# Where the weight combinations stand in VectorE's queue: behind the low part of the first half of the tile ahead

## The chip, the core and the metric

The kernel runs on one core of one Trainium2 chip. The metric is the device time of one execution in microseconds (us), lower is better. TensorE (PE in the profile, PEld for its weight loads), VectorE (DVE), ScalarE (ACT), GpSimd (POOL) and SyncE (SP, which issues most DMAs) each run their own queue of instructions in order.

## The reference

One layer of a hybrid block on 512 positions of width 2048, in float32: a norm, one wide input projection, two branches, and projections back.

```python
h = rmsnorm(x, norm1_w)
proj = einsum('bsd,de->bse', h, w_in)            # 2048 x 22592
q, k, v, g_ret, z, xbc, dt_raw, gate_r, gate_s = split(proj, offsets)
y_r = retention(q, k, v, positions) * silu(g_ret)          # 8 heads of 256
y_s = rmsnorm(ssd(xbc, dt_raw, ...) * silu(z), ssd_norm_w) # 64 heads of 64
merged = sigmoid(gate_r) * (y_r @ w_br_ret) + sigmoid(gate_s) * (y_s @ w_br_ssd)
return rmsnorm(x + merged @ w_out, norm_f_w)
```

Almost all of the arithmetic is in products of the activations (512 columns, kept transposed) with weight matrices.

## The kernel before

**A unit.** The function `unit` (L250) makes 256 output rows: a sum over 2048 inputs, taken in 8 steps k of 256 inputs. In most units a step is not the plain product of a 2x2 block matrix but the seven products of Strassen's scheme in Winograd's form (the table SEVEN): four 128x128 weight blocks are combined to seven, the activations likewise, and seven products of 128x128 by 128x256 stand for eight. Units called `plain` use the four blocks as they are, with 512 columns (FOUR).

**High and low parts.** Each float32 factor is split in a rounded high part and the rest, and each product is three matmuls: high by high (L213), high by low (L214), low by high (L215). So a seven-product step is 21 matmuls, a unit 168.

**What prepares the weights.** In `products` (L200) a weight tile `wf` (L221, three buffers) holds the blocks of two steps, its two halves. SP loads it with two DMAs (L227). VectorE makes the combinations of both halves at once with three instructions: L230 (two differences, 128x512), L232 (from the result of L230, 128x256) and L233 (from the result of L232, 128x256). Then for each half `split` (L147) lets ScalarE round it to `whi` (L148, 128x896, seven buffers) and VectorE subtract to get `wlo` (L149, 128x896, six buffers). ScalarE's rounding of a half reads all seven blocks, so it waits for L233; VectorE's low part waits for ScalarE's rounding of that half. A buffer of `wf` is free for the next load when the low part of its second half has been made; `whi` and `wlo` buffers when TensorE has done with that step.

**The order on TensorE in a unit.** Steps 0 to 4 run one after another; the last three steps (LAST, L245) run group by group, so that the accumulators `pb` or `att` end in three portions. Behind each portion VectorE and ScalarE combine the accumulators to the output `o` (L266 to L270).

**What sets the order.** The program is written without an order between units of work; the framework's scheduler lays the queues out, by priority and by its own model of when things end. The weights' preparation runs with a raised priority (`tc.high_priority(offset=PRIO)`, L219), so it stands ahead of where it is written. Once laid out, each queue's order is fixed. An ordering edge without a semaphore (`add_manual_dep` with NoSync, used so far by the class `InOrder`, L93) makes one instruction stand behind another in the same queue and costs no instruction.

**The stages.** A start (norm, rotary tables, first splits); retention, eight heads of four units (q, k, v, gate), with rotations, scores and group norms between; the SSD branch, eight groups g of seven units (B and C; x and z for two pairs of channel blocks; two gate units), with the convolutions (L590), scans (L635 to L675) and gates between; `w_br_ret`; the upper and the lower half of `w_br_ssd`, the latter with the merge (L726 to L729); `w_out` with the last norm. Each of the last four begins with new activations to be split, and runs a plain unit, six seven-product units and another plain unit (`w_out` ends in a form of its own).

Of the kernel before, what the change touches and what calls it, by code (L numbers as in the profile page):

```python
# [8 lines left out]
F32 = mybir.dt.float32  # L9
# [3 lines left out]
ALU = mybir.AluOpType  # L13
# [3 lines left out]
P = 128  # L17
# [110 lines left out]
def hybrid_block(tc, A, out):  # L128
    nc = tc.nc
    PE, ACT, DVE, POOL, SP = nc.tensor, nc.scalar, nc.vector, nc.gpsimd, nc.sync  # L130
# [6 lines left out]
    op = ctx.enter_context(tc.tile_pool(name="op", bufs=2))  # L137
# [8 lines left out]

    def split(dst_hi, dst_lo, src):  # L147
        ACT.copy(dst_hi, src)  # L148
        DVE.tensor_tensor(dst_lo, src, dst_hi.bitcast(F32), op=ALU.subtract)  # L149

# [8 lines left out]
    def high(k, x):  # L161
        return X[k][0][:, x, :] if isinstance(x, slice) or x < 4 else X[k][1][:, x - 4, :]

    def low(k, x):
        if isinstance(x, slice):
            return X[k][0][:, x.start + 4:x.stop + 4:x.step, :]
        return X[k][0][:, x + 4, :] if x < 4 else X[k][1][:, x - 1, :]
# [9 lines left out]
    def second_halves(room):  # L177

        for i in range(NP):
            f, g = R[i], room[i % 2]  # L180
            DVE.tensor_tensor(g[:, 0:2, :], f[:, 0:5:4, :], f[:, 2:3, :].to_broadcast([P, 2, 256]), op=ALU.add)
            DVE.tensor_tensor(g[:, 2, :], f[:, 3, :], g[:, 1, :], op=ALU.subtract)
            t = X[i][1] = hp.tile([P, 6, 256], F32R, name=f"b{i}", tag=f"b{i}")
            split(t[:, 0:3, :], t[:, 3:6, :], g)

    def pair_rows(f):
        return f[:, 0:4, :].rearrange("p (r h) t -> p r (h t)", r=2)

    def rows(src, i):
        return src[i * 256:(i + 1) * 256, :].rearrange("(r p) t -> p r t", p=P)  # L190
# [9 lines left out]
    def products(parts, pt, groups, PE=PE, after=None):  # L200


        started, ws = set(), []
        plain = groups is not SEVEN
        n = 4 if plain else 7

        def go(k, p):
            b, half, w, x = p
            hi, lo = ws[k]
            xh, xl = high(k, x), low(k, x)  # L210
            wh, wl = hi[:, w, :], lo[:, w, :]
            o = pt[b][:, half, :]
            PE.matmul(o, wh, xh, start=b not in started, stop=False, skip_group_check=True)  # L213
            PE.matmul(o, wh, xl, start=False, stop=False, skip_group_check=True)  # L214
            PE.matmul(o, wl, xh, start=False, stop=(k == NP - 1), skip_group_check=True)  # L215
            started.add(b)

        for k in range(NP):
            with tc.high_priority(offset=PRIO):  # L219
                if k % 2 == 0:  # L220
                    f2 = wp.tile([P, 2, 7, P], F32, name="wf", bufs=FB)  # L221
                    for m in range(2):
                        c = 0
                        v = pair_rows(f2[:, m])
                        for ap in parts:
                            w = ap.shape[-1]
                            SP.dma_start(out=v[:, :, c:c + w], in_=rows(ap, k + m))  # L227
                            c += w
                    if not plain:
                        DVE.tensor_tensor(f2[:, :, 4:6, :], f2[:, :, 1:3, :],  # L230
                                          f2[:, :, 0:1, :].to_broadcast([P, 2, 2, P]), op=ALU.subtract)
                        DVE.tensor_tensor(f2[:, :, 0, :], f2[:, :, 2, :], f2[:, :, 4, :], op=ALU.add)  # L232
                        DVE.tensor_tensor(f2[:, :, 6, :], f2[:, :, 3, :], f2[:, :, 0, :], op=ALU.subtract)  # L233
                f = f2[:, k % 2]
                hi = wp.tile([P, 7, P], F32R, name="whi", bufs=HB)
                lo = wp.tile([P, 7, P], F32R, name="wlo", bufs=LB)
                split(hi[:, :n, :], lo[:, :n, :], f[:, :n, :])
            ws.append((hi, lo))
            if k < NP - LAST:
                for g in groups:  # L240
                    for p in g:
                        go(k, p)
            if after and k == 1:
                after()
        for g in groups:  # L245
            for k in range(NP - LAST, NP):
                for p in g:
                    go(k, p)

    def unit(parts, alt=False, plain=False):  # L250

        if alt:
            pt = [att_tile().rearrange("p (h t) -> p h t", h=2) for b in range(4)]
        else:
            pt = [acc.tile([P, 2, 256], F32, name=f"pb{b}") for b in range(4)]
        products(parts, pt, FOUR if plain else SEVEN)
        o = op.tile([P, 4, 256], F32, name="o")
        with tc.high_priority():
            if plain:
                for c in range(2):  # L260
                    ACT.copy(o[:, 2 * c:2 * c + 2, :], pt[2 * c][:, 0:1, :].to_broadcast([P, 2, 256]))
                    DVE.tensor_tensor(o[:, 2 * c, :], pt[2 * c][:, 1, :], o[:, 2 * c, :], op=ALU.add)
                    DVE.tensor_tensor(o[:, 2 * c:2 * c + 2, :], pt[2 * c + 1], o[:, 2 * c:2 * c + 2, :], op=ALU.add)
            else:
                p1, u = o[:, 0, :], o[:, 0:4:3, :]
                ACT.copy(p1, pt[0][:, 0, :])  # L266
                DVE.tensor_tensor(o[:, 1:3, :], pt[1], p1[:, None, :].to_broadcast([P, 2, 256]), op=ALU.add)
                DVE.tensor_tensor(u, o[:, 2:3, :].to_broadcast([P, 2, 256]), pt[2], op=ALU.subtract)
                DVE.tensor_tensor(o[:, 2, :], o[:, 0, :], pt[2][:, 1, :], op=ALU.subtract)
                DVE.tensor_tensor(u, pt[3], u, op=ALU.add)  # L270
        flat = o.rearrange("p s t -> p (s t)")
        return flat[:, 512:], flat[:, :512]
# [212 lines left out]
    with tc.tile_pool(name="ret", bufs=1) as rp:  # L485
# [3 lines left out]
        for h in range(NH):  # L489
# [40 lines left out]
            for sb in range(TB):  # L530
                n = T - sb * P
# [38 lines left out]
    with tc.tile_pool(name="ssd", bufs=1) as sp:  # L570
# [30 lines left out]
        for g in range(NG):  # L601
# [14 lines left out]
            for jj in range(2):  # L616
# [5 lines left out]
                for e in range(2):  # L622
# [9 lines left out]
                    for c in range(TB):  # L632
# [6 lines left out]
                                       op=ALU.mult)  # L639
# [96 lines left out]
    with tc.tile_pool(name="fin", bufs=1) as fp:  # L736
# [50 lines left out]

        last_w = [w_o[:, D - 256:]]
        products(last_w, pt, PASSES[0], pe)
        t1, t0 = (t[:, :, h] for h in halves)  # L790
        act.copy(o[0][:, 0:2, :], pt[0])
        dve.tensor_tensor(t1, pt[1], t1, op=ALU.add)
        dve.tensor_tensor(t1, o[0][:, 0:2, :], t1, op=ALU.add)
        act.activation(o[0][:, 2:4, :], t1, AF.Square)
        dve.tensor_tensor(t0, o[0][:, 0:2, :], t0, op=ALU.add)
        products(last_w, pt, PASSES[1], pe, lambda: sums(0))
        finish(0)
        dve.tensor_tensor(t0, pt[2], t0, op=ALU.add)
# [44 lines left out]
```

## Time and profile before

| | |
|---|---|
| median of 3 runs | 2768.85 us (2766.91 to 2770.41) |
| the profiled execution's own time | 2769.07 us |
| its span, first to last instruction | 2767.2 us |
| TensorE busy | 2699.1 us, 98% of the span |
| TensorE's weight loads busy | 2567.6 us, 93% |
| VectorE busy | 2371.0 us, 86% |
| ScalarE busy | 1343.0 us, 49% |
| mean granted TensorE clock | 0.992 |

The execution lies 1.9 us above its span, and 0.2 us above the median of the runs. In the rows of the profile L149 is line 149 of the kernel; "out<-in" are tile names; "[0.35 <-ACT whi L148]" is idle time of the engine just before the instruction, and what ended it. In a row by window each engine has its busy time and its count of instructions; in a row of waits stand the total in us, the number of waits and the longest.

### The profile page before, as it was taken

The page shows a single profiled execution, that of the slowest core. Times are in us where ns is not written, and L with a number is a line of the kernel's source. Part 1 is how long each engine was busy: PE and PEld are TensorE (multiplying, and loading weights), DVE is VectorE, ACT ScalarE, POOL GpSimd, SP SyncE. Part 2 cuts the span into 40 slices and gives each one's busy share as a digit, 9 for nine tenths or more (in the row PEclk, how much of TensorE's full clock was granted, in tenths as well). Part 3 has the DMA queues.
Part 4 walks back from the last instruction along what each step waited for, and adds up shares of the span by engine and source line. Part 5 has one row for each costly group of instructions (what it writes and reads, how often), then busy time and mean ns, then how long its engine had stood idle before and what let it go on. Part 6 is the DMA issues. An engine that isn't in the chain of part 4 may idle for free.

```text
span 2767.2 us, 51984 instructions
## 1 busy us (share of the span) xinstructions
PE 2699.1 (98%) x20448; PEld 2567.6 (93%) x20448; DVE 2371.0 (86%) x3799; ACT 1343.0 (49%) x1923; POOL 175.2 (6%) x130
## 2 busy tenths in 40 slices
PE   6999999999999999999999999999999999999998
PEld 3799999999999999999999999999999989899898
DVE  8788888888878898898989888898889798898997
ACT  4334333343336555566565556556564353433453
POOL 0000000000000100000000000000000000011221
PEclk8999999999999999999999999999999999999999
DMA  4233333333333434343443434344464544557634
GB/s 141 77 96 92 115 100 107 96 100 103 104 112 107 141 108 127 121 129 121 128 142 120 136 108 128 116 132 126 131 200 144 192 155 141 179 169 230 203 123 138
DMA packets 339766, 362.46 MB, mean 131 GB/s; under 512 B 25152, under 2 KB 297792, under 8 KB 339520
## 3 DMA queue, kind: packets, MB, share of 16 engines
q1 hardware_dynamic: 319136, 325.05, 38.2%
q10 hardware_dynamic: 20384, 34.09, 3.3%
q8 instruction: 160, 2.62, 0.4%
q14 instruction: 86, 0.70, 0.1%
HBM read 321.56 MB, written 37.49 MB: 130 GB/s over the span
## 4 chain that ended last, share of the span: by engine, by line
PE 75%; DVE 11%; DMA 8%; issue 3%; ACT 1%; SPq 1%; POOL 0%; DVEq 0%; ACTq 0%; POOLq 0%
PE pb L215 21%; PE pb L214 21%; PE pb L213 20%; DVE wlo L149 3%; DMA wf<-in_w_in_dram 3%; DMA wf<-in_w_br_ssd_dram 2%; PE att L215 2%; PE att L214 2%; PE att L213 2%; PE att L549 1%; PE att L534 1%; DVE wf L230 1%; PE att L666 1%; PE pb L118 1%; PE att L670 1%
## 5 line engine op out<-in xcount | busy, mean ns | idle before, releaser
L148 ACT CAST whi<-wf 128x896 fp32r<-128x896 f32 (+1 forms) x968 | 818.5, 884 | 925.8 <-PE pb L214 390.0
L149 DVE TENSOR_TENSOR wlo<-wf,whi 128x896 fp32r<-128x896 f32 (+1 forms) x968 | 989.9, 1034 | 64.4 <-ACT whi L148 33.3
L213 PE MATMUL pb<-a,whi 128*128 128x256 f32 (+1 forms) x3328 | 1001.8, 304 | 13.7 <-ACT a L118 9.4
L214 PE MATMUL pb<-a,whi 128*128 128x256 f32 (+1 forms) x3328 | 1002.4, 302 | 8.7 <-DVE a L118 8.7
L215 PE MATMUL pb<-a,wlo 128*128 128x256 f32 (+1 forms) x3328 | 999.6, 302 | 5.9 <-DVE wlo L149 5.9
L213 PEld LDWEIGHTS pb<-a,whi 128*128 128x128 f32 x3328 | 636.7, 192 | 41.5 <-ACT a L118 13.3
L214 PEld LDWEIGHTS pb<-a,whi 128*128 128x128 f32 x3328 | 639.1, 192 | 33.9 <-DVE a L118 12.8
L215 PEld LDWEIGHTS pb<-a,wlo 128*128 128x128 f32 x3328 | 637.9, 192 | 29.9 <-DVE wlo L149 7.7
L213 PE MATMUL pb<-b,whi 128*128 128x256 f32 x2112 | 599.6, 284 | 0.0
L215 PE MATMUL pb<-b,wlo 128*128 128x256 f32 x2112 | 598.8, 284 | 0.0
L214 PE MATMUL pb<-b,whi 128*128 128x256 f32 x2112 | 598.0, 284 | 0.0
L230 DVE TENSOR_TENSOR wf<-wf 128x512 f32<-128x512 f32 x400 | 286.2, 715 | 185.3 <-DMA wf<-in_w_in_dram 138.7
L214 PEld LDWEIGHTS pb<-b,whi 128*128 128x128 f32 x2112 | 405.4, 192 | 0.1
L215 PEld LDWEIGHTS pb<-b,wlo 128*128 128x128 f32 x2112 | 405.3, 192 | 0.2
L213 PEld LDWEIGHTS pb<-b,whi 128*128 128x128 f32 x2112 | 405.4, 192 | 0.0
L233 DVE TENSOR_TENSOR wf<-wf 128x256 f32<-128x256 f32 x400 | 175.5, 439 | 3.4
L232 DVE TENSOR_TENSOR wf<-wf 128x256 f32<-128x256 f32 x400 | 174.5, 436 | 3.6
L215 PE MATMUL att<-a,wlo 128*128 128x256 f32 (+1 forms) x480 | 144.6, 306 | 5.3 <-DVE wlo L149 5.3
L213 PE MATMUL att<-a,whi 128*128 128x256 f32 (+1 forms) x480 | 145.5, 305 | 0.0
L214 PE MATMUL att<-a,whi 128*128 128x256 f32 (+1 forms) x480 | 145.3, 305 | 0.0
L215 PEld LDWEIGHTS att<-a,wlo 128*128 128x128 f32 x480 | 91.0, 192 | 10.3 <-DVE wlo L149 6.5
L659 ACT ACTIVATE L<-L,sst 128x128 f32<-128x128 f32 x256 | 78.5, 390 | 35.8 <-DMA L<-A_d 35.8
(221 smaller groups left out, 2736.6 us busy)
## 6 DMA issues: line engine op xcount, KB each, us to landing
wf<-in_w_in_dram SPq DMA_DIRECT2D x640, 256.0 KB, 3.1
wf<-in_w_br_ssd_dram SPq DMA_DIRECT2D x128, 256.0 KB, 3.4
wf<-in_w_out_dram SPq DMA_DIRECT2D x72, 256.0 KB, 3.2
wf<-in_w_in_dram SPq DMA_DIRECT2D x128, 128.0 KB, 2.6
L<-A_d SPq DMA_DIRECT2D x32, 512.0 KB, 3.7
wf<-in_w_br_ret_dram SPq DMA_DIRECT2D x64, 256.0 KB, 3.4
ys_d<-B ACTq DMA_DIRECT2D x32, 256.0 KB, 2.1
r<-ys_d SPq DMA_DIRECT2D x16, 512.0 KB, 6.1
```

The source lines that it names most:

```text
L118: ins = getattr(self.engine, name)(*args, **kw).ins
L148: ACT.copy(dst_hi, src)
L149: DVE.tensor_tensor(dst_lo, src, dst_hi.bitcast(F32), op=ALU.subtract)
L213: PE.matmul(o, wh, xh, start=b not in started, stop=False, skip_group_check=True)
L214: PE.matmul(o, wh, xl, start=False, stop=False, skip_group_check=True)
L215: PE.matmul(o, wl, xh, start=False, stop=(k == NP - 1), skip_group_check=True)
L230: DVE.tensor_tensor(f2[:, :, 4:6, :], f2[:, :, 1:3, :], f2[:, :, 0:1, :].to_broadcast([P, 2, 2, P]), op=ALU.subtract)
L232: DVE.tensor_tensor(f2[:, :, 0, :], f2[:, :, 2, :], f2[:, :, 4, :], op=ALU.add)
L233: DVE.tensor_tensor(f2[:, :, 6, :], f2[:, :, 3, :], f2[:, :, 0, :], op=ALU.subtract)
L534: PE.matmul(ps[:, :n], k[:, i, sb * P:(sb + 1) * P], q[:, i, sb * P:], start=(i == 0), stop=(i == 1))
L549: PE.matmul(ps[:, :DK], pt[sb][:, (lb - sb) * P:(lb - sb + 1) * P], v[:, sb, :], start=(sb == 0), stop=(sb == lb))
L659: ACT.activation(L[:, i, c, :], L[:, i, c, :], AF.Relu, scale=-1.0, bias=At[:, c, h0 + i:h0 + i + 1])
```

## The change

The low part's instruction is noted for every half of every tile (the list `lows`, in order of the program). The first of the three combinations of a tile is given an ordering edge: it stands behind the low part noted last but one, which is that of the first half of the tile ahead. The edge carries no semaphore and no arithmetic changes. The other two combinations follow through their data. In the changed kernel the three combinations are L239, L244 and L245 (before: L230, L232, L233), and the output's are L279 to L282 (before: L267 to L270); the merge's L727 to L729 are L739 to L741.

```diff
     def split(dst_hi, dst_lo, src):
         ACT.copy(dst_hi, src)
-        DVE.tensor_tensor(dst_lo, src, dst_hi.bitcast(F32), op=ALU.subtract)
+        return DVE.tensor_tensor(dst_lo, src, dst_hi.bitcast(F32), op=ALU.subtract).ins.name
+
+    lows = []
+
+    def behind(ins, other):
+
+        tc.add_manual_dep(
+            ins, other,
+            mybir.DependencyInfo(mybir.DependencyClass.NoSync, mybir.DependencyReason.DATA),
+            reason="order of issue")
...
                     if not plain:
-                        DVE.tensor_tensor(f2[:, :, 4:6, :], f2[:, :, 1:3, :],
-                                          f2[:, :, 0:1, :].to_broadcast([P, 2, 2, P]), op=ALU.subtract)
+                        first = DVE.tensor_tensor(f2[:, :, 4:6, :], f2[:, :, 1:3, :],
+                                                  f2[:, :, 0:1, :].to_broadcast([P, 2, 2, P]), op=ALU.subtract)
+
+                        if len(lows) > 1:
+                            behind(first.ins, lows[-2])
                         DVE.tensor_tensor(f2[:, :, 0, :], f2[:, :, 2, :], f2[:, :, 4, :], op=ALU.add)
                         DVE.tensor_tensor(f2[:, :, 6, :], f2[:, :, 3, :], f2[:, :, 0, :], op=ALU.subtract)
...
-                split(hi[:, :n, :], lo[:, :n, :], f[:, :n, :])
+                lows.append(split(hi[:, :n, :], lo[:, :n, :], f[:, :n, :]))
```

The scheduler lays the queues out anew under this edge. First place: VectorE's queue in the retention stage, within a unit, before; wf_3263 and wf_3319 are two tiles that follow wf_3112, and each L149 row makes the low part of one half of the tile it reads.

```order
L230 TENSOR_TENSOR wf_3263<-wf_3263 128x2x256
L232 TENSOR_TENSOR wf_3263<-wf_3263 128x2x128
L233 TENSOR_TENSOR wf_3263<-wf_3263 128x2x128
L149 TENSOR_TENSOR wlo_3119<-wf_3112,whi_3118 128x896
L230 TENSOR_TENSOR wf_3319<-wf_3319 128x2x256
L149 TENSOR_TENSOR wlo_3123<-wf_3112,whi_3122 128x896
L232 TENSOR_TENSOR wf_3319<-wf_3319 128x2x128
L149 TENSOR_TENSOR wlo_3270<-wf_3263,whi_3269 128x896
L233 TENSOR_TENSOR wf_3319<-wf_3319 128x2x128
L149 TENSOR_TENSOR wlo_3295<-wf_3263,whi_3294 128x896
```

The same tiles on VectorE in the changed kernel, combinations now L239, L244 and L245.

```order
L149 TENSOR_TENSOR wlo_3119<-wf_3112,whi_3118 128x896
L239 TENSOR_TENSOR wf_3263<-wf_3263 128x2x256
L149 TENSOR_TENSOR wlo_3123<-wf_3112,whi_3122 128x896
L244 TENSOR_TENSOR wf_3263<-wf_3263 128x2x128
L245 TENSOR_TENSOR wf_3263<-wf_3263 128x2x128
L149 TENSOR_TENSOR wlo_3270<-wf_3263,whi_3269 128x896
L239 TENSOR_TENSOR wf_3319<-wf_3319 128x2x256
L149 TENSOR_TENSOR wlo_3295<-wf_3263,whi_3294 128x896
```

Before, all three combinations of wf_3263 stood ahead of both low parts of wf_3112; now the first stands between these two, and the third right ahead of the low part of its own tile's first half.

Second place: VectorE's queue at the end of a unit in the stage of the lower half of `w_br_ssd`, before; o_27521 is the output of the unit that ends, L729 the last instruction of a merge, and the tiles from wf_27553 on belong to the unit that follows (wlo_27560, ahead of the rows shown, and wlo_27585 are its steps 0 and 1).

```order
L149 TENSOR_TENSOR wlo_27585<-wf_27553,whi_27584 128x896
L267 TENSOR_TENSOR o_27521<-pb1_27294,o_27521 128x512
L729 TENSOR_TENSOR f_27282<-f_27282,f_27286 128x512
L149 TENSOR_TENSOR wlo_27616<-wf_27609,whi_27615 128x896
L233 TENSOR_TENSOR wf_27665<-wf_27665 128x2x128
L149 TENSOR_TENSOR wlo_27641<-wf_27609,whi_27640 128x896
L268 TENSOR_TENSOR o_27521<-o_27521,pb2_27295 128x2x256
L230 TENSOR_TENSOR wf_27700<-wf_27700 128x2x256
L149 TENSOR_TENSOR wlo_27672<-wf_27665,whi_27671 128x896
L269 TENSOR_TENSOR o_27521<-o_27521,pb2_27295 128x256
L149 TENSOR_TENSOR wlo_27697<-wf_27665,whi_27696 128x896
```

The same end of a unit on VectorE in the changed kernel, the output's instructions now L279 to L282.

```order
L149 TENSOR_TENSOR wlo_27560<-wf_27553,whi_27559 128x896
L239 TENSOR_TENSOR wf_27609<-wf_27609 128x2x256
L149 TENSOR_TENSOR wlo_27585<-wf_27553,whi_27584 128x896
L279 TENSOR_TENSOR o_27521<-pb1_27294,o_27521 128x512
L244 TENSOR_TENSOR wf_27609<-wf_27609 128x2x128
L280 TENSOR_TENSOR o_27521<-o_27521,pb2_27295 128x2x256
L245 TENSOR_TENSOR wf_27609<-wf_27609 128x2x128
L281 TENSOR_TENSOR o_27521<-o_27521,pb2_27295 128x256
L282 TENSOR_TENSOR o_27521<-pb3_27296,o_27521 128x2x256
L149 TENSOR_TENSOR wlo_27616<-wf_27609,whi_27615 128x896
```

Before, six low parts of the unit that follows stood ahead of the last combination of the output (L270, two rows behind those shown); now two do, and the four combinations of the output stand with no low part between them.

Counted over the whole queue (400 tiles with combinations): before, the first combination stood two or more low parts ahead of its tile's own first low part in 387 cases; now it stands exactly one ahead in all 400. The third stood one or more ahead in 317 cases before; now it stands ahead of no other low part in 389. Between it and its own first low part stands no instruction at all in 180 of the 400 (before: in none).

## The prediction

> **What bounds the kernel now.** First the page's busy times and the head of the chain that ended last.
>
> ```profile
> PE 2699.1 (98%) x20448; PEld 2567.6 (93%) x20448; DVE 2371.0 (86%) x3799; ACT 1343.0 (49%) x1923; POOL 175.2 (6%) x130
> PE 75%; DVE 11%; DMA 8%; issue 3%; ACT 1%; SPq 1%; POOL 0%; DVEq 0%; ACTq 0%; POOLq 0%
> ```
>
> TensorE is idle for only 2767.2 - 2699.1 = 68 us, so no change of order can win more than that. An average over stages says little, so next the stretches: start, one head of retention, two groups of the SSD branch, `w_br_ret`, the two halves of `w_br_ssd`, `w_out`. The columns are the stretch, its length, and busy time and instruction count of PE, PEld, DVE, ACT and POOL.
>
> ```profile
> 0.00:60.00 60.00, 38.17 (x110) 18.57 (x110) 48.78 (x83) 27.22 (x35) 0.33 (x6) 0.91 0.49 156
> 60.00:85.00 25.00, 18.00 (x46) 11.98 (x47) 22.59 (x38) 12.04 (x16) 0.00 (x0) 0.73 0.11 36
> 401.00:492.00 91.00, 91.00 (x726) 88.89 (x726) 76.63 (x131) 34.35 (x45) 3.11 (x4) 1.00 0.34 102
> 1302.00:1617.00 315.00, 314.57 (x2492) 303.05 (x2491) 276.13 (x432) 185.98 (x285) 21.93 (x16) 1.00 0.41 126
> 2100.00:2200.00 100.00, 100.00 (x835) 100.00 (x835) 84.26 (x131) 38.75 (x47) 0.00 (x0) 1.00 0.48 157
> 2260.00:2370.00 110.00, 108.90 (x905) 108.49 (x905) 89.41 (x134) 41.73 (x51) 1.57 (x1) 1.00 0.47 150
> 2420.00:2540.00 120.00, 111.99 (x905) 110.04 (x903) 108.53 (x161) 41.30 (x52) 18.70 (x10) 0.99 0.58 181
> 2680.00:2740.00 60.00, 59.98 (x501) 59.78 (x500) 51.65 (x69) 31.40 (x47) 12.46 (x8) 1.00 0.40 124
> ```
>
> Of the 68 us, 21.8 + 7.0 = 29 lie in the first 85 us, where no tile has combinations. The long stages run at TensorE's pace: 835 matmuls in 100 us are 0.120 us each, so a unit of 168 takes 20.1 us, a tile (two steps) 5.0. VectorE follows at 84 to 88% in the retention, the SSD branch and `w_br_ret`, and 90% in the lower half of `w_br_ssd` (2420 to 2540), where TensorE is idle for 8.0 us.
>
> Third, TensorE's waits from 85 to 2600 us, the longest.
>
> ```profile
> PE att L215 <- DVE wlo L149: 5.3, 5, 1.8
> PE pb L215 <- DVE wlo L149: 5.3, 4, 2.7
> PE pb L213 <- DVE o L269: 4.0, 7, 1.2
> ```
>
> TensorE waits for VectorE's low parts and, at a unit's switch, for an accumulator. So VectorE's queue is the resource the change acts on, and where it has little to spare decides.
>
> **The change: what goes.** VectorE's idle time before, by what ended it (two SSD groups first, then the lower half of `w_br_ssd`).
>
> ```profile
> DVE wf L230 <- DMA wf<-in_w_in_dram: 19.3, 27, 1.3
> DVE wlo L149 <- ACT whi L148: 7.4, 4, 3.4
> DVE B L590 <- ACT B L587: 2.7, 3, 0.9
> DVE L L662 <- ACT L L661: 0.9, 1, 0.9
> DVE wf L230 <- DMA wf<-in_w_br_ssd_dram: 8.6, 8, 4.0
> DVE f L728 <- POOL f L726: 2.4, 2, 1.2
> ```
>
> The first combination, at the head of the queue, waits for its DMA, with low parts behind it that could run. It now stands about one tile's VectorE work later, so these waits should mostly go. SP's order hardly changes, and a buffer of `wf` is still freed by the low part of a tile's second half.
>
> **What comes.** Combination, rounding and low part now follow each other without a tile between. What that chain takes can be read where it already happens, in `w_br_ret`; DVE rows first, then ACT's.
>
> ```profile
> 2182.13 0.41 DVE L233 TENSOR_TENSOR wf<-wf 128x256 f32<-128x256 f32 x1
> 2182.47 0.42 DVE L232 TENSOR_TENSOR wf<-wf 128x256 f32<-128x256 f32 x1
> 2182.92 0.42 DVE L233 TENSOR_TENSOR wf<-wf 128x256 f32<-128x256 f32 x1
> 2183.69 1.09 DVE L149 TENSOR_TENSOR wlo<-wf,whi 128x896 fp32r<-128x896 f32 x1 [0.35 <-ACT whi L148]
> 2187.10 0.69 DVE L230 TENSOR_TENSOR wf<-wf 128x512 f32<-128x512 f32 x1 [2.32 <-DMA wf<-in_w_br_ret_dram]
> 2187.71 1.08 DVE L149 TENSOR_TENSOR wlo<-wf,whi 128x896 fp32r<-128x896 f32 x1
> 2188.71 0.42 DVE L232 TENSOR_TENSOR wf<-wf 128x256 f32<-128x256 f32 x1
> 2189.05 1.08 DVE L149 TENSOR_TENSOR wlo<-wf,whi 128x896 fp32r<-128x896 f32 x1
> 2190.05 0.42 DVE L233 TENSOR_TENSOR wf<-wf 128x256 f32<-128x256 f32 x1
> ```
>
> ```profile
> 2182.71 3.46 ACT L148 CAST whi<-wf 128x896 fp32r<-128x896 f32 x4 [7.20 <-DVE wf L233]
> ```
>
> The third combination starts at 2182.13, the rounding at 2182.71, the low part at 2183.69: 1.56 us. The combination occupies VectorE for 0.41, so with nothing between, VectorE stands idle for 1.15 us; each us of other work between saves as much. A combination right behind the one it reads starts 0.45 us after it (2182.47 to 2182.92), with another instruction between, 0.34 (2188.71 to 2189.05). So an empty place costs 1.15 + 0.11 = 1.26 us, and a place with L281 and L282 in it (0.93 of pitch: 0.33 + 0.60) 0.22.
>
> The Trainium skill says otherwise on the small part (VectorE: DVE Perf Modes, section The DRAIN you can't avoid): chained instructions cost the same with a semaphore between as without. The 0.45 against 0.34 here disagrees, and the measurement decides; by the page the 0.11 fall away, and the sum below would be some 8 us smaller.
>
> Whether these waits show depends on the stage: VectorE's busy time per unit, plus them, against TensorE's time per unit.
>
> - Start, plain units: no combinations, 0.
> - Retention: of a head's 16 tiles 8 places are empty, four partly filled (1.1 us): 8 x 1.26 + 1.1 = 11.2. 76.6 + 11.2 = 87.8 of 91 us: covered by the slack in which VectorE now waits, so 0; it costs at most 1 us a head (7) if bursts of the rotation exceed the lead.
> - SSD: per group of 157.5 us, 276.13/2 = 138.1 busy; of 24 places 10 are empty (12.6) and seven partly filled (3.4). Waits on ScalarE and its chains stay, (7.4 + 2.7 + 0.9)/2 = 5.5. Sum 159.6, or 155.9 if the 3.7 of waits for `whi` are the same waits: between 2.1 over and 1.6 under. I take half of the excess, 1.2 a group, 8 x 1.2 = 10 us.
> - `w_br_ret`: 84.26% of 20.1 is 16.9 a unit, three empty places and one with L281 and L282 (4.0): 20.9, 0.8 over; six units, 5 us.
> - Upper half of `w_br_ssd`: 89.41/110 x 20.1 = 16.3, + 4.0 = 20.3: 0.2 over, six units 1.2, against 1.1 of idle TensorE there that goes with the DMA waits: 0.
> - Lower half: 905/168 = 5.4 units in 120 us, 22.3 each; busy 20.1. One empty place, one with L281 and L282, two with a merge instruction (0.54 each): 2.6, and 0.4 for the wait on POOL (2.4/5.4). 23.1 - 22.3 = 0.8, six units, 5 us: the DMA waits that go are outweighed.
> - `w_out`: 51.65/60 x 20.1 = 17.3, + 4.0 = 21.3: 1.2 over, five units, 6 us.
> - The output's combinations have no low parts (1.0 us each) between them any more, so the 4.0 us for L269 should halve: -2.
>
> Sum: 10 + 5 + 5 + 6 - 2 = 24 us. Against the execution's own 2769.07 that is 2793; it lies 0.2 us above the median, so no correction.
>
> What covers the waits is the lead, and it shrinks: at a unit's end two low parts of the next unit are ready, not five or six. Two steps are 5 us of TensorE's work. In a unit without other work the third low part starts at once behind the output, so that holds; with convolutions or scans in front it may not, which is the upward part of the range.
>
> A row on shared work: in the lower half POOL is busy for 18.70 of 120 us. The Trainium skill states (SBUF — State Buffer, section Who interferes with whom) that a VectorE instruction with two inputs in SBUF and a GpSimd instruction that reads SBUF exclude each other, and the one issued first wins. No row quoted here shows it; by that rule VectorE's new idle time would cover a little of POOL's, under 1 us in all by estimate.
>
> **The rivals.** A measurement tells about 0.2% (5.5 us) from no change.
>
> - *Faster (18%).* The new waits fall into the time in which VectorE waited for DMAs, and TensorE's waits for low parts (5.3 + 5.3) and half of L269's go: 2769 - 12.6 = 2756. For it: the DMA waits, 9.7 us a group in the SSD branch, are about as much as 12.6 of empty places. It decides if, in the lower half of `w_br_ssd`, VectorE's unit stays under 20.1; against it, it is busy for 20.1 already.
> - *No change (14%).* The waits are paid from slack everywhere and nothing is won: 2769. That the order might not change at all is excluded by the order itself.
> - *Much slower (20%).* In the SSD branch the rounding, now wanted at once, stands behind ScalarE's scan work:
>
> ```profile
> 1032.93 2.45 ACT L659 ACTIVATE L<-L,sst 128x128 f32<-128x128 f32 x8
> 1037.86 1.28 ACT L661 ACT_TABLE_LOAD   x1
> 1039.15 1.06 ACT L661 ACTIVATE L<-L 128x1024 f32<-128x1024 f32 x1
> ```
>
>   That is 2.45 + 1.28 + 1.06 = 4.8 us a scan, 32 scans; were a quarter of it to reach TensorE, 38 us more: 2831. It decides once the wait per group passes the 157.5 - 155.9 us left.
>
> **How the numbers follow.** The forecast as summed has 48%: 2793, its own range 2776 to 2812 (SSD at 0 or at 2.1 a group and retention at 7, each with the other terms, rounded outward). The range over the cases goes from 2757 to 2836: below it lies about half of the faster case (9%), above it half of the much slower one (10%). Slower by over 0.2%: 48 + 20 = 68%; within: 14%; faster: 18%.
>
> **What would show it right or wrong.** VectorE's waits over the whole span before, of the first combination on DMAs and of the low part on ScalarE:
>
> ```profile
> DVE wf L230 <- DMA wf<-in_w_in_dram: 138.7, 165, 2.7
> DVE wlo L149 <- ACT whi L148: 33.3, 26, 4.2
> DVE wf L230 <- DMA wf<-in_w_br_ssd_dram: 25.4, 21, 4.0
> DVE wf L230 <- DMA wf<-in_w_br_ret_dram: 14.0, 12, 2.4
> DVE wf L230 <- DMA wf<-in_w_out_dram: 4.5, 5, 1.5
> ```
>
> L239's waits on DMAs, 138.7 + 25.4 + 14.0 + 4.5 = 183 us before as L230's, fall below 40; L149's on ScalarE, 33 us before, pass 150, in pieces near 1.15. TensorE's idle time grows in the lower half of `w_br_ssd`, in `w_out` and in the SSD branch, by waits of L215 on low parts, and not in retention. If L149's waits grow but TensorE's idle time doesn't, the slack was larger than the rows say; if DMA waits stay, the loads and not the queue set them; if the growth sits in retention, the shrunken lead decides.

## The result and the profile after

The changed kernel takes 2872.44 us (median of 4 runs, 2866.88 to 2874.95) against 2767.88 for the kernel before: ratio 1.0379, 95% interval 1.0365 to 1.0394. It is slower by 105 us where 24 were forecast, beyond the range's upper end of 2836.

First the page's busy times of the changed kernel.

```profile
PE 2746.4 (96%) x20448; PEld 2585.2 (90%) x20448; DVE 2372.0 (83%) x3799; ACT 1347.9 (47%) x1925; POOL 163.2 (6%) x130
```

The profiled execution took 2866.88 us, the shortest of the four. Its span grew from 2767.2 to 2865.1 us, by 97.9. TensorE's idle time grew from 68.1 to 118.7, by 50.6. The other 47.3 are growth of its *busy* time, for the same 20448 matmuls. VectorE's busy time is unchanged (2371.0 and 2372.0): the order cost no work, only waiting.

Where the time went, by stage. TensorE's matmuls with weights are the same 18,816 in the same stages in every kernel here, so a stage can be cut at the start of its first one (numbers 5161, 13921, 15121, 16321 and 17521, from 168 per seven-product unit and 96 per plain unit). The retention is counted from the first matmul with weights, `w_out` to the start of the last. The differences are taken before rounding.

| us | retention | SSD | `w_br_ret` | `w_br_ssd` upper | lower | `w_out` |
|---|---|---|---|---|---|---|
| before | 762.0 | 1274.4 | 164.5 | 167.0 | 176.1 | 175.5 |
| changed | 762.4 | 1347.0 | 172.5 | 167.8 | 183.4 | 184.6 |
| more | 0.4 | 72.5 | 8.0 | 0.8 | 7.3 | 9.0 |
| forecast | 0 | 10 | 5 | 0 | 5 | 6 |

The stretches of the changed kernel that answer to those shown of before: one head of retention, two groups of the SSD branch, and the four last stages, whole.

```profile
401.30:492.30 91.00, 91.00 (x727) 88.88 (x726) 76.00 (x131) 34.45 (x45) 3.87 (x4) 1.00 0.33 102
1279.30:1617.80 338.50, 324.62 (x2488) 306.80 (x2489) 276.05 (x432) 185.80 (x282) 19.33 (x16) 0.99 0.39 118
2142.40:2314.80 172.40, 169.41 (x1200) 160.93 (x1201) 147.08 (x228) 71.48 (x93) 0.00 (x0) 0.97 0.50 165
2314.80:2482.70 167.90, 166.07 (x1204) 157.58 (x1204) 139.31 (x215) 70.32 (x92) 1.51 (x1) 1.00 0.48 157
2482.70:2666.00 183.30, 171.30 (x1201) 158.59 (x1200) 158.80 (x240) 67.40 (x88) 21.07 (x14) 1.00 0.61 194
2666.00:2850.60 184.60, 174.49 (x1302) 167.05 (x1301) 160.65 (x234) 83.19 (x117) 32.90 (x14) 0.98 0.39 127
```

The head still takes 91 us. Two SSD groups take 338.5 us instead of 315, with VectorE busy for the same 276 us.

VectorE's waits for the rounding in the whole span, and the group of the first combination, whose last figure is the idle time ahead of it.

```profile
DVE wlo L149 <- ACT whi L148: 233.3, 225, 2.9
```

```profile
L239 DVE TENSOR_TENSOR wf<-wf 128x512 f32<-128x512 f32 x400 | 276.7, 692 | 0.0
```

The DMA waits (183 us before) are gone entirely, and 200 us of waits for the rounding (33 before) have taken their place. Two tiles in the SSD branch, each with an empty place, on VectorE's timeline:

```profile
1379.97 0.41 DVE L244 TENSOR_TENSOR wf<-wf 128x256 f32<-128x256 f32 x1
1380.42 0.43 DVE L245 TENSOR_TENSOR wf<-wf 128x256 f32<-128x256 f32 x1
1381.94 1.09 DVE L149 TENSOR_TENSOR wlo<-wf,whi 128x896 fp32r<-128x896 f32 x1 [1.09 <-ACT whi L148]
1382.95 0.68 DVE L239 TENSOR_TENSOR wf<-wf 128x512 f32<-128x512 f32 x1
1383.55 1.08 DVE L149 TENSOR_TENSOR wlo<-wf,whi 128x896 fp32r<-128x896 f32 x1
1384.55 0.41 DVE L244 TENSOR_TENSOR wf<-wf 128x256 f32<-128x256 f32 x1
1385.00 0.42 DVE L245 TENSOR_TENSOR wf<-wf 128x256 f32<-128x256 f32 x1
1386.48 1.09 DVE L149 TENSOR_TENSOR wlo<-wf,whi 128x896 fp32r<-128x896 f32 x1 [1.05 <-ACT whi L148]
```

The gap is 1.09 and 1.05 us, and L245 starts 0.45 after L244: both prices of the prediction (1.15 and 0.45). Over the whole span 180 of the 225 waits, one for each empty place, stand right behind a third combination; they make 207.0 of the 233.3 us, 1.15 each.

TensorE's longest waits for work of the new order:

```profile
PE pb L222 <- ACT whi L148: 28.3, 27, 3.0
PE pb L224 <- DVE wlo L149: 21.4, 34, 1.2
```

It waits more for roundings than for low parts: a step's first matmul needs only the high part, and that now comes late too.

### The profile page after: what moved, and what is told of

It reads as the page before. It is cut to its first block, busy times and chain, and to the rows that moved or that the text cites. A ratio compares the mean times of both kernels' runs of the same rounds, so it can differ in the third digit from the quotient of the medians.

```text
span 2865.1 us, 51557 instructions
## 1 busy us (share of the span) xinstructions
PE 2746.4 (96%) x20448; PEld 2585.2 (90%) x20448; DVE 2372.0 (83%) x3799; ACT 1347.9 (47%) x1925; POOL 163.2 (6%) x130
## 4 chain that ended last, share of the span: by engine, by line
PE 73%; DVE 14%; ACT 4%; DMA 4%; issue 3%; POOL 0%; SPq 0%; ACTq 0%; DVEq 0%; POOLq 0%
PE pb L224 20%; PE pb L222 20%; PE pb L223 19%; DVE wlo L149 4%; PE att L222 3%; PE att L224 3%; PE att L223 3%; DMA L<-A_d 2%; DVE wf L239 2%; ACT whi L148 2%; ACT L L671 1%; PE att L561 1%; PE att L546 1%; DVE B L602 1%; PE att L678 1%
## 5 line engine op out<-in xcount | busy, mean ns | idle before, releaser
L149 DVE TENSOR_TENSOR wlo<-wf,whi 128x896 fp32r<-128x896 f32 (+1 forms) x968 | 1000.4, 1039 | 273.0 <-ACT whi L148 233.3
L222 PE MATMUL pb<-a,whi 128*128 128x256 f32 (+1 forms) x3328 | 972.4, 306 | 51.2 <-ACT whi L148 28.3
L223 PE MATMUL pb<-a,whi 128*128 128x256 f32 (+1 forms) x3328 | 966.2, 302 | 8.6 <-DVE a L118 8.6
L224 PE MATMUL pb<-a,wlo 128*128 128x256 f32 (+1 forms) x3328 | 951.5, 305 | 21.6 <-DVE wlo L149 21.4
L224 PEld LDWEIGHTS pb<-a,wlo 128*128 128x128 f32 x3328 | 614.0, 193 | 56.5 <-DVE wlo L149 30.3
L239 DVE TENSOR_TENSOR wf<-wf 128x512 f32<-128x512 f32 x400 | 276.7, 692 | 0.0
L245 DVE TENSOR_TENSOR wf<-wf 128x256 f32<-128x256 f32 x400 | 177.4, 444 | 6.0
L244 DVE TENSOR_TENSOR wf<-wf 128x256 f32<-128x256 f32 x400 | 173.6, 434 | 0.1
L222 PE MATMUL att<-a,whi 128*128 128x256 f32 (+1 forms) x480 | 137.9, 306 | 6.0 <-ACT whi L148 5.8
L223 PE MATMUL att<-a,whi 128*128 128x256 f32 (+1 forms) x480 | 137.2, 304 | 0.0
L224 PE MATMUL att<-a,wlo 128*128 128x256 f32 (+1 forms) x480 | 133.6, 307 | 1.1 <-DVE wlo L149 0.9
L222 PEld LDWEIGHTS att<-a,whi 128*128 128x128 f32 x480 | 91.6, 191 | 11.5 <-ACT whi L148 7.6
```

What stands on the lines that cost most here:

```text
L149: return DVE.tensor_tensor(dst_lo, src, dst_hi.bitcast(F32), op=ALU.subtract).ins.name
L239: first = DVE.tensor_tensor(f2[:, :, 4:6, :], f2[:, :, 1:3, :], f2[:, :, 0:1, :].to_broadcast([P, 2, 2, P]), op=ALU.subtract)
```

## The experiments

Three theories. **E**: the empty places, in which VectorE stands idle for the rounding, are what costs. **L**: the number of low parts that are ready at a unit's switch (five or six before, two now) is what costs. **Of the SSD branch alone**, **A**: ScalarE's scan work stands in front of the roundings; **D**: the scans' loads of the decay tile `L` come late, and ScalarE stands at the head of its queue for them.

**Two by two: empty places and lead.** The first kernel fills the empty places: the low part of the second half of the tile ahead is put behind the third combination (`lows` holds the instructions here).

```diff
-                        DVE.tensor_tensor(f2[:, :, 6, :], f2[:, :, 3, :], f2[:, :, 0, :], op=ALU.subtract)
+                        third = DVE.tensor_tensor(f2[:, :, 6, :], f2[:, :, 3, :], f2[:, :, 0, :], op=ALU.subtract)
+                        if lows:
+                            behind(lows[-1], third.ins.name)
```

> The changed order, and one more edge a tile: the low part of the second half of the tile ahead stands behind the third combination, so the first combination stays where the change put it (exactly one low part ahead of its own), but no tile has its third combination right ahead of its own low part (180 of 400 in the changed kernel). At a unit's end three to five low parts of the next unit stand ahead of the output's last combination (mostly two in the changed kernel, five to six before). Theory E (VectorE's idle time in the empty places is what costs): back at the time before, 2765 to 2775 us, with VectorE's waits for ScalarE's rounding below 90 us (233 in the changed kernel). Theory L (the number of low parts ready at a unit's switch is what costs): part of the way, 2785 to 2820, TensorE still waiting at the switches of the scan units. Theory A (rounding held up by ScalarE's scan work): the 25 us outside the SSD branch go, most of the 73 in it stay: 2825 to 2850.

Measured: 2745.31 us, ratio 0.9932 (0.9915 to 0.9948). It is faster than the kernel before. VectorE's waits in it:

```profile
DVE o L281 <- PE pb L224: 48.8, 45, 2.6
DVE wlo L149 <- PE pb L224: 47.9, 58, 3.0
DVE wlo L149 <- ACT whi L148: 44.4, 46, 3.3
```

The waits for the rounding are back at 44 us, and VectorE now waits mostly for TensorE, which means that it is ahead. (In this kernel lines stand two further down: L281 is the output's first combination.) L and A had 2785 and more; E's lowest was 2765, so this time is 20 us under it too.

The second has no empty places either, but the lead at a unit's end is held at two, as in the changed kernel (added to the first; `ends` holds the last output combination):

```diff
+                if k == 2 and ends:
+                    behind(lows[-1], ends.pop().name)
```

> As the kernel with the third combination ahead of the second half's low part, and the third low part of a unit behind the last output combination of the unit ahead of it, so at a unit's end mostly two low parts of the next unit are ready (86 of 103 unit ends), as in the changed kernel, but no place is empty. Theory E: still near the time before, 2765 to 2785. Theory L: nearly as slow as the changed kernel, 2840 to 2875. Theory A: 2825 to 2860.

Measured: 2783.63 us, ratio 1.0067 (1.0052 to 1.0082): within E's range, 56 us under L's lowest. The third keeps the changed kernel's empty places and gives it a lead of five:

```diff
+                if k == 4 and ends:
+                    behind(ends.pop(), lows[-1])
```

> The changed order with its empty places (178 of 400), but the last output combination of a unit stands behind the fifth low part of the next unit, so five are ready at a unit's end, as before the change. Theory E: about as slow as the changed kernel, 2850 to 2875. Theory L: most of the loss goes, 2770 to 2795. Theory A: 2835 to 2870, the rounding being as late as in the changed kernel.

Measured: 2869.53 us, ratio 1.0382 (1.0366 to 1.0397): as slow as the changed kernel. VectorE's waits for the rounding are no fewer than the changed kernel's 233.3 us, and TensorE's no fewer than its 28.3:

```profile
DVE wlo L149 <- ACT whi L148: 276.6, 256, 4.2
```

```profile
PE pb L222 <- ACT whi L148: 43.9, 37, 2.1
```

So at a lead of two the empty places cost 2872 - 2784 = 89 us; a lead of five buys nothing while they are there, and 38 us (2784 - 2745) once they are gone. E holds, L is at most second. With the places filled the order is better than before the change, so the later place of the first combination was itself no loss. An empty place does two things: VectorE stands idle, and the rounding that TensorE's step begins with comes later. Filling it mends both, and no run tells them apart.

**The distance of the edge.** The same edge, one line changed: on the low part one, three or four back (two back is the change).

```diff
-                        if len(lows) > 1:
-                            behind(first.ins, lows[-2])
+                        if len(lows) > 2:
+                            behind(first.ins, lows[-3])
```

> The edge of the change on the low part noted three back in place of two: the first combination stands exactly two low parts ahead of its own in 397 of 400 tiles, the third is always at least two instructions ahead of its own low part, and five to six low parts of the next unit are ready at a unit's end. All three theories: the loss goes. E and L: 2760 to 2775, VectorE's waits of the first combination on DMAs (183 us before) below 80 us and its waits for the rounding near the 33 us of before. A: 2770 to 2790.

Measured: 2740.08 us, ratio 0.9911 (0.9896 to 0.9926), 25 us faster than the kernel before and the best order found. The page's busy times, and the first combination's group:

```profile
PE 2686.5 (98%) x20448; PEld 2562.5 (94%) x20448; DVE 2352.6 (86%) x3799; ACT 1328.2 (49%) x1910; POOL 189.7 (7%) x130
```

```profile
L239 DVE TENSOR_TENSOR wf<-wf 128x512 f32<-128x512 f32 x400 | 295.2, 738 | 50.3 <-DMA wf<-in_w_in_dram 28.8 <-DMA wf<-in_w_br_ret_dram 10.1 <-DMA wf<-in_w_br_ssd_dram 8.3
```

The forecast of all three theories was too high by 20 us and more. None had counted that the DMA waits, 183 us before and 50 here, might cost TensorE something; whether that is the gain is not shown. By stage against before: SSD 1254.6 (-19.8), lower half 169.9 (-6.2), `w_out` 173.3 (-2.2), the others within 1.6.

> The edge on the low part noted four back: the first combination stands one to three low parts ahead of its own (before the change up to four), in one of 400 tiles the third has a single instruction behind it, in none is the place empty, four to six low parts are ready at unit ends. No empty places, so by theory E no loss: between the kernel with the edge three back (2740) and the one before (2765); VectorE's waits for the weights' DMAs between their 47 and 183 us. If those waits are what the gain of the edge three back came from, the time stands with them: 2745 to 2765.

Measured: 2749.82 us, ratio 0.9946 (0.9927 to 0.9965). The time is where it was expected, but it doesn't stand with the DMA waits:

```profile
DVE wf L239 <- DMA wf<-in_w_in_dram: 103.0, 122, 2.6
DVE wf L239 <- DMA wf<-in_w_br_ssd_dram: 19.6, 18, 2.7
DVE wf L239 <- DMA wf<-in_w_br_ret_dram: 12.8, 9, 2.6
DVE wf L239 <- DMA wf<-in_w_out_dram: 1.6, 2, 0.9
```

Together 137 us: a quarter of the 183 is gone, and more than half of the gain (16 of 25 us) is there. The kernel with the places filled has only 1 us of these waits and gains 20. So the gain doesn't follow their sum, and where it comes from is open.

> The edge of the change on the low part noted last in place of last but one: all three combinations of a tile stand behind both low parts of the tile ahead. 236 of 400 places are empty (180 in the changed kernel), and two low parts are ready at most unit ends, as there. Theory E: slower than the changed kernel, by up to 56 more empty places of 1.2 us (67 us) and more where all three combinations now fall into the same wait: 2890 to 2960 us. Theory L: the lead is as in the changed kernel, so 2865 to 2880.

Measured: 2943.28 us, ratio 1.0653 (1.0633 to 1.0674): 71 us over the changed kernel, as E had it, where L had none. Distances one, two, three and four back give 2943, 2872, 2740 and 2750 us, with 236, 180, 0 and 0 empty places.

**Inside the SSD branch.** Four kernels that leave work out, so their times stand only against each other: the 32 loads of `L` (the scan's activations read a constant tile), and the loads with ScalarE's work on `L` (VectorE multiplies a constant), each in the changed order and in the one before.

```diff
-                    SP.dma_start(out=L.rearrange("p i c l -> p i (c l)"),
-                                 in_=A_d[hs, :].partition_broadcast(P))
...
-                            ACT.activation(L[:, i, c, :], L[:, i, c, :], AF.Relu, scale=-1.0,
+                            ACT.activation(L[:, i, c, :], ident, AF.Relu, scale=-1.0,
```

> The changed order, with the 32 loads of the decay tile L of a scan left out (the eight activations of a scan read a constant tile instead, so ScalarE does the same work but waits for no DMA; 100 us of such waits in the SSD branch in the changed kernel). The SSD branch took 72.5 us longer in the changed kernel than before. Compared with the same left out of the order before: theory E (empty places alone): still 60 to 80 us more in the SSD branch. Theory D (the loads come late, ScalarE stands for them at the head of its queue and the roundings behind it): 35 us or less. Theory A (ScalarE's own scan work ahead of the roundings): 50 to 75.

> The control for the loads of L: the kernel before with the same 32 loads left out. All theories: 2755 to 2769, the SSD branch within 10 us of the 1274 us before, since ScalarE waits for these loads for 36 us there and TensorE for almost nothing behind them.

> The changed order, with the loads of L and ScalarE's whole work on it left out (eight activations, one more over 128x1024, and most table loads: about 4.8 us a scan); VectorE's multiplication reads a constant tile, in two instructions. Against the same left out of the order before, in the SSD branch: theory E: still 60 to 80 us more. Theory D: 35 or less, and no less than with the loads alone left out. Theory A: 35 or less here, but 50 to 75 with the loads alone left out.

> The control: the kernel before with the loads of L and ScalarE's work on it left out. All theories: 2745 to 2769, the SSD branch 0 to 20 us shorter than the 1274 before.

Measured (one run each): 2828.62 and 2756.42 us without the loads, 2818.87 and 2747.96 without the work. In the SSD branch:

| us | changed order | order before | difference |
|---|---|---|---|
| whole | 1347.0 | 1274.4 | 72.5 |
| without the loads | 1311.9 | 1260.8 | 51.1 |
| without loads and ScalarE's work | 1299.5 | 1256.8 | 42.7 |

No theory had its number: E said 60 to 80 in both rows, D at most 35, A at most 35 in the last. The loads carry 21 us of the 72.5, ScalarE's work 8, and 43 stay with neither. These are single runs, and the changed kernel's own four runs span 8.1 us: the 8 is no more than that, the 21 and the 43 are well above it. The order before lost 13.6 to the loads, where 10 at most were expected. What the loads do is seen on ScalarE in the changed kernel, its wait and then the queue behind it:

```profile
ACT L L671 <- DMA L<-A_d: 100.5, 30, 6.8
```

```profile
1356.49 2.45 ACT L671 ACTIVATE L<-L,sst 128x128 f32<-128x128 f32 x8 [4.84 <-DMA L<-A_d]
1358.85 1.77 ACT L148 CAST whi<-wf 128x896 fp32r<-128x896 f32 x2
```

Two roundings stand behind an activation that waits 4.84 us for its load. Before, ScalarE's waits for these loads were 36 us; with the places filled they are 37, and 66 with the lead held at two as well. So the late loads go along with late scans and add to them; that they follow from them is argued and not shown.

**Do they come late by their queue?** The loads issued by ScalarE's queue, where no weight load stands ahead of them, in the order with the edge three back and in the changed one.

```diff
-                    SP.dma_start(out=L.rearrange("p i c l -> p i (c l)"),
+                    ACT.dma_start(out=L.rearrange("p i c l -> p i (c l)"),
```

> The edge three back (2740 us), and the 32 loads of L issued by ScalarE's queue in place of SyncE's, where weight loads that wait for a buffer stand ahead of them. ScalarE waits for these loads for 39 us in the kernel with the edge three back. If those waits come from what stands ahead on SyncE's queue and still cost TensorE time: 2725 to 2737. If TensorE is covered there already: 2738 to 2743. If the waits for L's buffer now hold up ScalarE's queue: 2745 to 2770.

Measured: 2740.96 us, ratio 0.9912 (0.9897 to 0.9926): the same as on SyncE's queue, with 36 us of waits for the loads instead of 39.

> The changed kernel (180 empty places), with the 32 loads of L issued by ScalarE's queue in place of SyncE's; nothing is left out. Leaving these loads out took 21 us from what the change costs in the SSD branch (72.5 to 51.1 against the same left out of the order before). If they come late because weight loads that wait for a buffer stand ahead of them on SyncE's queue: ScalarE's waits for them fall from 100 us to below 50 and the time to 2845 to 2858. If they come late because L itself is still read by TensorE when the next scan wants it: the waits stay (as waits of ScalarE's queue or of its activations) and the time stays within 2860 to 2880. Theory E expects no less than 2840 in any case, the empty places being the same.

Measured: 2880.28 us, ratio 1.0412 (1.0395 to 1.0430), 82 us of waits for the loads instead of 100. That is 0.3 us over the range for an `L` that is still in use, and far over the range for SyncE's queue (2845 to 2858). Taking the loads off SyncE's queue wins nothing, so that queue isn't the reason. That `L` is still in use is what remains: what SyncE waits for with the load of `L` in the SSD branch of the changed kernel is TensorE's last reading of the `L` before.

```profile
SPq L667 <- PE att L678: 117.1, 30, 5.6
```

A second buffer for `L`, which would settle it, wasn't tried.

## Why the prediction was wrong

**Right.** The direction; the prices of an empty place; that the DMA waits go; that retention and the upper half pay from slack (0.4 and 0.8 us); that TensorE's idle time grows in the SSD branch (11.7 to 50.1 us), in the lower half (8.0 to 12.0) and in `w_out` (4.4 to 10.1) and not in the retention, though more of it behind roundings than behind low parts. The lower half is 7.3 for 5: its empty places cost 11.6 at an equal lead (183.4 against 171.8 with the places filled), and the rest of the change won 4.3. `w_out`, 9.0 for 6, is in part luck: with the places filled and the lead at two it takes 184.8, with the places empty and a lead of five 185.7, with the places filled and a longer lead 173.7. There the shorter lead alone costs as much, and the sum had only the places.

**The step that failed** is the SSD term, "276.13/2 = 138.1 busy; of 24 places 10 are empty (12.6) and seven partly filled (3.4)", set against "per group of 157.5 us" and so to "1.2 a group, 8 x 1.2 = 10 us". It measured 72.5/8 = 9.1 a group, which is 62.5 of the 97.9 - 24 = 74 us by which the profiled execution missed the forecast. (Half of the excess of 2.1 is 1.05 and not 1.2, and the terms give 2783 to 2807 for the range of 2776 to 2812; these slips are small beside that.) VectorE's waits in this stage of the changed kernel, the largest:

```profile
DVE wlo L149 <- ACT whi L148: 113.5, 112, 2.9
DVE E L685 <- PE att L682: 22.4, 9, 2.8
DVE o L279 <- PE pb L224: 19.3, 14, 2.0
DVE wlo L149 <- PE pb L224: 15.0, 18, 1.7
```

The new waits weren't priced too low: 16.0 a group were forecast, and all waits for roundings measured 113.5/8 = 14.2. Of these, 66.4/8 = 8.3 a group show in the time at an equal lead (1347.0 for the changed kernel, 1280.6 with the places filled and the lead at two). What failed is that VectorE's other idle time in the group was counted as slack that pays for them. A group took 1347.0/8 = 168.4 us: 138.0 of work, 14.2 of waits for roundings, and 16.2 of other idle time, for which the sum had (2.7 + 0.9)/2 = 1.8. Most of it is waiting for TensorE, 10.1 a group where it was 4.2 before.

One group by unit shows where that slack is missing. First the changed kernel's first gate unit, then its last two units (the second z and the second gate) together:

```profile
1344.90:1370.70 25.80, 25.80 (x232) 25.20 (x231) 20.31 (x37) 13.11 (x23) 3.43 (x3) 1.00 0.39 120
1392.30:1446.30 54.00, 50.17 (x402) 46.60 (x400) 45.73 (x74) 33.38 (x52) 4.54 (x4) 1.00 0.38 111
```

The same units where the empty places are filled:

```profile
1315.40:1341.10 25.70, 25.70 (x231) 25.10 (x230) 24.45 (x42) 15.25 (x26) 4.79 (x3) 1.00 0.46 141
1361.30:1407.50 46.20, 46.20 (x402) 45.60 (x401) 41.75 (x67) 27.56 (x45) 3.06 (x3) 1.00 0.40 120
```

In the first gate unit VectorE does 20.3 us of work where it does 24.5 with the places filled, since it waits there for 2.8 us for a product of a scan and 2.7 for roundings. TensorE doesn't notice, but VectorE leaves 4 us of work to the units that follow. In the last two, TensorE has the same 402 matmuls in both kernels. VectorE has 45.7 us of work where it has 41.8 with the places filled, and waits for 8.0, of which 6.4 are for roundings. That makes 53.7 of the 54.0 us which these units take instead of 46.2. The seven groups that have a first gate unit agree: VectorE works in it for 20.0 us on average (24.3 with the places filled), and the last two units take 55.0 (46.2). Idle time in one unit is not carried to the next: it is work put off. This is read from the traces; no run changes it alone.

**The rivals.** "Much slower" named ScalarE's scan work, 4.8 us a scan of which a quarter reaches TensorE: 38 us. That work is worth 8 at most, the loads ahead of it, which it didn't name, 21. Its sign and stage were right; its size was too small (10 + 38 = 48 us for 72.5), and most of the loss has another cause. "Faster" (2756, the new waits hidden in the time of the DMA waits) is refuted for the changed order. Orders with no empty places and a lead of more than two do gain (2740 to 2750 us), but as their gain doesn't follow the DMA waits, that is no proof of its reason.

**Smaller terms.** The 4.0 us for the output's third combination didn't halve (L281: 3.8), and L278 added 4.3:

```profile
PE pb L222 <- ACT o L278: 4.3, 6, 1.2
PE pb L222 <- DVE o L281: 3.8, 6, 1.2
```

In `w_br_ret` the 8.0 us are not what was summed. VectorE's queue there, at one place:

```profile
2274.83 0.42 DVE L244 TENSOR_TENSOR wf<-wf 128x256 f32<-128x256 f32 x1
2277.44 0.42 DVE L182 TENSOR_TENSOR r<-r 128x256 f32<-128x256 f32 x1 [2.20 <-DMA r<-ys_d]
2277.79 0.68 DVE L190 TENSOR_TENSOR g<-r 128x512 f32<-128x512 f32 x1
2278.39 0.42 DVE L245 TENSOR_TENSOR wf<-wf 128x256 f32<-128x256 f32 x1
```

An addition of the next stage's activations waits 2.20 us for its load, between the second and the third combination of a tile that TensorE wants at once. TensorE's wait behind it is 2.98 us and has an aftermath (below, 2.6 us by estimate). With another wait of 1.9, for an output, that is 7.5 of the 8.0. With the places filled the stage takes 164.5, as before.

**The bound.** "TensorE is idle for only 2767.2 - 2699.1 = 68 us, so no change of order can win more" treated busy time as fixed. It moved from 2686.5 us (the edge three back) to 2768.6 (one back) over these orders, for the same matmuls.

## What to carry to other kernels

Where a queue has little to spare, two dependent instructions of it with another engine's step between them must have work in between, and an ordering edge has to be judged by what ends up in that place. Count the new waits against the slack of each unit and not of the whole group: idle time that comes a unit too early pays for nothing. Where a profile shows an instruction waiting at the head of its queue, moving it by one place more or less (here three back in place of two) can turn a loss of 3.8% into a gain of 0.9%.

## What the runs showed of the hardware

**A wait costs TensorE more than its length.** TensorE after a short wait, in the changed kernel:

```profile
1444.82 0.28 PE L224 MATMUL pb<-b,wlo 128*128 128x256 f32 x1
1446.35 0.39 PE L222 MATMUL pb<-a,whi 128*128 128x256 f32 x1 [1.25 <-ACT o L278]
1446.57 0.28 PE L223 MATMUL pb<-a,whi 128*128 128x256 f32 x1
```

The first matmul takes 0.39 us and the next starts 0.22 behind it, where the pace is 0.12. After the long wait in `w_br_ret`:

```profile
2279.89 0.58 PE L222 MATMUL pb<-a,whi 128*128 128x256 f32 x1 [2.98 <-ACT whi L148]
2280.27 0.41 PE L223 MATMUL pb<-a,whi 128*128 128x256 f32 x1
2280.48 0.41 PE L222 MATMUL pb<-a,whi 128*128 128x256 f32 x1
```

```profile
2279.00:2286.00 7.00, 6.11 (x27) 5.82 (x28) 5.46 (x11) 2.99 (x4) 0.00 (x0) 0.53 0.73 245
```

For 7 us the granted clock is 0.53 and matmuls start 0.21 apart. By estimate the 6.11 us of matmuls would have taken 6.11 x 0.12 / 0.21 = 3.5 at the usual pace, so this costs 2.6 us more. The Trainium skill (TensorE: Matmul & The Clock Gate, section Part 1: The HAM clock gate) states that an idle window of some 3.4 us halves the clock and that at least one busy window of that length restores it. The row agrees in the halving; here a wait of 2.98 us was enough, and the half clock lasted for some 7 x 0.47 / 0.5 = 6.6 us, about two such windows. All of this is booked as busy. A lower clock can make only a part of the 47.3 us: with a mean granted clock of 0.988 over 2865.1 us and 0.992 over 2767.2, the clock withheld is worth 34 and 22 us, so at most some 12 more. The rest was not separated.

**VectorE stands beside some of GpSimd's work.** GpSimd and VectorE in the changed kernel:

```profile
1440.92 1.36 POOL L692 TENSOR_TENSOR R<-R,B 128x512 f32<-128x512 f32 x1 [7.31 <-ACT B L691]
```

```profile
1441.05 2.19 DVE L149 TENSOR_TENSOR wlo<-wf,whi 128x896 fp32r<-128x896 f32 x1
```

The low part takes 2.19 us instead of 1.08 where it overlaps a GpSimd addition, the wait showing as duration. In the changed kernel 21 of the 968 low parts take over 1.5 us, and each of them overlaps a GpSimd instruction of this kind (over 128x384 or 128x512); beside GpSimd's powers over 128x1 (L567) a low part keeps its 1.08. The Trainium skill (SBUF — State Buffer, section Who interferes with whom) states that the port pair which VectorE and GpSimd share is an exclusive lock. The prediction quoted no row for it, and this is one that agrees; the kernel before has such rows too (2.19 us at 1726.07).
